# Six stores of normed activations move from ScalarE's queue, in the norm, to the load queue, in the attention

## The chip, the core and the metric

The kernel runs on one core of a Trainium2 chip. A core has five engines that work side by side, each with its own stream of instructions: TensorE (PE in the profile, with its weight loads as PEld), VectorE (DVE), ScalarE (ACT), GpSimd (POOL) and SyncE (SP), which here only issues transfers. Sixteen DMA engines move data between HBM and the on-chip memory SBUF, and within SBUF; a transfer is issued by an instruction on one of the engines' streams. Engines meet at semaphores: an instruction waits until the instructions or transfers that it depends on have counted up.

The metric is the device time of one execution in microseconds, lower is better.

## The reference

The kernel computes one step of a two-layer encoder over 1056 frames (1024 of a prompt, 32 of a sample), 1024 features wide, in float32. Cut to what matters:

```python
def trunk(x, ...):
    for layer in range(DEPTH):                       # 2
        if layer < N_A_LAYERS:                       # layer 0
            mix, C, n, m = mlstm_mixer(x, ...)
        else:                                        # layer 1
            kv = (x @ w_kv).reshape(B, T, 2, N_KV_HEADS, HEAD_DIM)
            k_sh, v_sh = kv[:, :, 0], kv[:, :, 1]
            mix = swa_prompt(x, k_sh, v_sh, w_q_b[j], sinks_b[j], w_out_b[j], slopes)   # or swa_sample
        x = layer_norm(DEEPNORM_ALPHA * x + mix, ln_g[layer, 0], ln_b[layer, 0])
        x = layer_norm(DEEPNORM_ALPHA * x + swiglu(x, w_gu[layer], w_down[layer]), ln_g[layer, 1], ln_b[layer, 1])
    return x, ...

def sink_attention(q, k, v, sinks, bias):
    s = jnp.einsum('bcqhgd,bckhd->bchgqk', q, k) * (HEAD_DIM ** -0.5) + bias
    ...
    return jnp.einsum('bchgqk,bckhd->bcqhgd', p, v)
```

The change lies where layer 0 ends and layer 1 begins: the second `layer_norm` of layer 0 gives the x of which layer 1 makes its keys, values and queries, and which it needs again later, as the residual `DEEPNORM_ALPHA * x + mix`. The attention has 16 query heads of 64 features and two shared key/value heads, over a window of 128 frames.

## The kernel before

**Data.** The activations lie in SBUF in one tile `ACT`, 128 partitions (features within a block) by 8 blocks by 1056 frames; the profile calls it `act`. Float32 products are made of three matmuls on halves: each operand is split into a high half (rounded by ScalarE) and a low half (the rest, by VectorE or GpSimd), and `gemm` adds high·high, low·high and high·low (L402 to L404). The halves of the activations are `SX` (`sx`, L511 and L517), those of the weights `wh` and `wl`, made from the loaded weights `wr` (load L163 on SP, high half L237 on ScalarE, low half L239 mostly on GpSimd).

**The norm (`ln_task`).** It works on quarters of the frames, 264 each. For each quarter it goes through the four pairs of feature blocks: VectorE multiplies by the inverse deviation, ScalarE applies gain and offset (L505), ScalarE writes the high half (L511), VectorE or GpSimd the low half (L517). After the feed-forward part of layer 0 (`li == 1`) a store follows the high half (L513): the attention overwrites `ACT` with its outputs, so the normed values go to `scr` in HBM (`scrx` in the profile) and come back as the residual (`mixed_parts`, L1211 and L1213). Four quarters by four pairs make 16 stores of 264 KB, all issued by ScalarE. They are ScalarE's only transfers.

**The attention.** `keys_values` projects the keys (`k_group`; `k_spread` then copies their halves `KH` and `KL` between partitions, L1623 to L1627 on SP) and the values (`v_group`, transposed by `v_turn`, L1736, and split into `VR`, L1678 and L1679). `q_group(j, g)` projects the queries of pair j of the heads and group g of the frames (groups of 384, 384 and 288): high half `qh` (L1657, ScalarE), low half `ql` (L1658, VectorE), and then four copies on SP which place both into `Q` (L1664 and L1665). `qh` and `ql` have two buffers each, so the third group made waits for the copies of the first. The scores are matmuls of `KH`, `KL` and `Q` (L1763, L1764); VectorE adds the bias `bt` (L1769), whose last column, the sink, GpSimd copies (L1697; L1698 for the sample's `sb`); then come the exponential on ScalarE (L1781), the scaling on GpSimd (L1787), transposes (L1807), products with `VR` (L1822, L1823) and the write to `act` (L1831, L1833).

**What sets the order.** The program is written out in one order for each engine. A class `Weave` holds cooperative tasks: `launch` adds one, `tick(us)` lets an assumed time pass and runs on every task whose pause is over, `drain` runs one to its end. A task yields the pause to its next step. So the pauses in the code fix where in each engine's stream an instruction stands, and nothing is reordered when the kernel runs. Weights are fed by the same ticks. SP's stream holds all loads, the copies within SBUF and the remaining stores; an issue that has to wait holds up everything behind it.

Of the kernel before, what the change touches and what calls it, by code (L numbers as in the profile page):

```python
# [65 lines left out]
HALF = T // 2  # L66
# [216 lines left out]
def kernel(ctx: ExitStack, tc: tile.TileContext, A, O):  # L283
    nc = tc.nc
    ctx.enter_context(tc.manual_schedule())
    wv = Weave()
# [11 lines left out]
    def new(p, tag, shape, dt=F32, bufs=1):  # L298
        uid[0] += 1
        return p.tile(list(shape), dt, name=f"{tag}_{uid[0]}", tag=tag, bufs=bufs)  # L300
# [72 lines left out]
    ACT = base.tile([P, KT, T], F32, name="act")  # L373
# [8 lines left out]
    scr = dram.tile([P, KT, T], F32, name="scrx")  # L382
# [56 lines left out]

    QUARTERS = [(group(g), (g % 2, slice(0, N4))) for g in range(4)]  # L440

    squared, added = set(), set()

    def ln_task(z_, lps, grp, li, last, final):
        cols, (c, zs) = grp
        w = cols.stop - cols.start

        rush = final and grp is QUARTERS[2]
        y = RUSH if rush else LN_PACE[li & 1][last]
        acc = z_[:, 0:2, c, zs]  # L450
        sq = [acc] + [z_[:, 2 + 2 * i : 4 + 2 * i, c, zs] for i in range(3)]
        rs, r2 = z_[:, 8, c, zs], z_[:, 9, c, zs]
        n = KT // 2

        def z2(kk):
            return ACT[:, 2 * kk : 2 * kk + 2, cols]

        def s2(i, kk):
            return SX[:, i, 2 * kk : 2 * kk + 2, cols]

        yield y[0]
        pm = new(lps, "ln", [P, 512], bufs=3 if li & 1 else 2)[:, :w]
        nc.tensor.matmul(pm, onesm[:], acc[:, 0, :], start=True, stop=True)
        yield y[1]
        for s in range(n + 2):
            if s < n:

                nc.vector.tensor_sub(z2(s), pm.unsqueeze(1).broadcast_to([P, 2, w]), z2(s))
            if 1 <= s <= n:
                nc.scalar.activation(sq[s - 1], z2(s - 1), AF.Square)  # L470
            if s >= 3:
                (nc.gpsimd if rush or li & 1 and not (last or s & 1) else nc.vector).tensor_add(acc, acc, sq[s - 2])
            yield y[2]
        if not rush:
            nc.vector.tensor_add(acc[:, 0], acc[:, 0], acc[:, 1])
        added.add((li, cols.start // N4))
        yield y[3] + LN_LAG.get((li, cols.start // N4), 0.0)
        pv = new(lps, "ln", [P, 512], bufs=3 if li & 1 else 2)[:, :w]
        for i in range(1 + rush):
            nc.tensor.matmul(pv, onesm[:], acc[:, i, :], start=(i == 0), stop=(i == rush))  # L480
        squared.add((li, cols.start // N4))
        yield y[4]

        if not li & 1:
            nc.scalar.preload_act_table_set("natural_log_exp_and_others")
        nc.scalar.activation(rs, pv, AF.Ln, bias=eps_ln[:])
        nc.scalar.activation(rs, rs, AF.Exp, scale=-0.5)
        nc.scalar.activation(r2, rs, AF.Square, scale=0.5 ** 0.5)
        yield y[5]
        nc.vector.scalar_tensor_tensor(r2, pv, eps_ln[:], r2, op0=ALU.add, op1=ALU.mult)  # L490
        nc.vector.scalar_tensor_tensor(rs, r2, 1.5, rs, op0=ALU.subtract, op1=ALU.mult)
        if (li, cols.start // N4) == (1, 2):
            while (1, 3) not in added:
                yield 0.2
        for s in range(n + 3):
            if s < n:
                nc.vector.tensor_mul(z2(s), z2(s), rs.unsqueeze(1).broadcast_to([P, 2, w]))
            kk = s - 1
            if 0 <= kk < n:
                for k in (2 * kk, 2 * kk + 1):  # L500
                    z, gk, bk = ACT[:, k, cols], lng[:, li, k : k + 1], lnb[:, li, k : k + 1]
                    if li & 1 and last and k & 1:
                        nc.vector.tensor_scalar(z, z, gk, bk, op0=ALU.mult, op1=ALU.add)
                    else:
                        nc.scalar.activation(z, z, AF.Identity, scale=gk, bias=bk)  # L505
            kk = s - 2
            if 0 <= kk < n:
                if final:
                    nc.sync.dma_start(O["y"][:, 2 * kk : 2 * kk + 2, cols], z2(kk))
                else:  # L510
                    nc.scalar.copy(s2(0, kk), z2(kk))  # L511
                    if li == 1:
                        nc.scalar.dma_start(scr[:, 2 * kk : 2 * kk + 2, cols], z2(kk))  # L513
            kk = s - 3
            if kk >= 0 and not final:
                eng = nc.gpsimd if kk & li & 1 else nc.vector
                eng.tensor_sub(s2(1, kk), z2(kk), s2(0, kk).bitcast(F32))  # L517
            yield y[6]
# [194 lines left out]
    cols = [pa.tile([P, 3, 96], F32, name=f"cols{g}") for g in range(3)]  # L713
# [485 lines left out]
    def mixed_parts(src, free, mixed, pauses):  # L1199


        for g in range(3):
            t0, n = GRP[g]
            while not free(g):
                yield 0.3
            for k in range(KT):
                while not mixed(k, g):
                    yield 0.3
                split_act(k, g)
                if g == 0:  # L1210
                    nc.sync.dma_start(act[k][g], src[:, k, t0 : t0 + n])  # L1211
                elif k % 4 == 3:
                    nc.sync.dma_start(act_g[g][:, k - 3 : k + 1], src[:, k - 3 : k + 1, t0 : t0 + n])  # L1213
                yield pauses[g]
            nparts[0] += 1
# [434 lines left out]
    def q_group(j, g):  # L1650

        t0, n = GRP[g]
        ps = project(U_QB[g > 0][j], g)
        q = Q[j, g] = new(pb, "Q", [P, 2, 384], F32R, bufs=4)
        h, l = (new(pb, tag, [P, 384], F32R, bufs=2)[:, :n] for tag in ("qh", "ql"))
        sc = -(HD ** -0.5)
        nc.scalar.activation(h, ps, AF.Copy, scale=sc)  # L1657
        nc.vector.scalar_tensor_tensor(l, ps, sc, h.bitcast(F32), op0=ALU.mult, op1=ALU.subtract)  # L1658

        def place():  # L1660
            yield 1.0
            for i in range(2):
                own, other = slice(64 * i, 64 * i + 64), slice(64 - 64 * i, 128 - 64 * i)
                nc.sync.dma_start(q[own, i, :n].bitcast(F32), h[own].bitcast(F32))  # L1664
                nc.sync.dma_start(q[other, i, :n].bitcast(F32), l[own].bitcast(F32))  # L1665

        return wv.launch(place())
# [34 lines left out]
    def keys_values(g):  # L1702
        if g == 2:
            k_part(ck[:], SEQ, P)
        for f, w in ((k_group, U_KV[g > 0][0]), (v_group, U_KV[g > 0][1])):
            f(g)
            if g != 1:
                W.done(w)
# [22 lines left out]
    def v_turn(group, pause):  # L1731
        yield pause
        for c, c0, L, g, off in CH:
            if g == group:
                pt = new(psb, "O", [P, 512], bufs=2)
                nc.tensor.transpose(pt[:L, :P], vT[g][:, off : off + L], ident[:])  # L1736
                v_parts(c, pt[:L, :P], L)
                ast["v"] = c + 1
                yield 0.8
# [119 lines left out]
    wv.launch(v_turn(0, 0))  # L1859
    task = wv.launch(attention((GAP_A,) * 8))  # L1860
    ast["ready"] = 4
    for g in range(1, 3):
        keys_values(g)
        wv.launch(v_turn(g, 2.5))
# [8 lines left out]
    def q_made():  # L1873
        yield 4.0
        ast["ready"] += 1

    for i, (j, g) in enumerate(QG):
        if i < 4:
            continue

        while ast["scored"] < 3 * (i - 3):
            wv.tick(0.25)
        q_group(j, g)
        wv.launch(q_made())
        if g == 2:
            W.done(U_QB[1][j])
        if (j, g) == (7, 0):
            nparts[0] = 0
            parts = wv.launch(
                mixed_parts(  # L1890
                    scr,
                    lambda g: ast["ready"] > QG.index((7, g)),
                    lambda k, g: ast["placed"] >= 3 * QG.index((k, g)) + 3,
                    (1.6, 1.0, 1.0),
                )
            )
# [145 lines left out]
```

## Time and profile before

| what | us |
|---|---|
| three timed executions | 2210.44, 2210.89, 2212.62 |
| median | 2210.89 |
| the profiled execution, whole | 2213.98 |
| its span (first to last instruction) | 2212.2 |
| TensorE busy in the span | 2175.5 |
| first and last issue of the stores of L513 | 1134.7, 1197.6 |
| first issue of a load of what they wrote (L1211) | 1342.9 |

Starts in the profile are counted from the span's start. In the rows that follow, an instruction has its start, its length, the engine (a q behind the engine's name: the issue of a transfer), line, operation, output and inputs; in brackets stands how long the engine had been idle and what released it. The chain of work is followed back from a last instruction, at each step to what released it. The transfers of SP take 40.0% of the sixteen DMA engines' span, those of ScalarE 0.6%:

```profile
q1 hardware_dynamic: 169936, 290.94, 40.0%
q10 hardware_dynamic: 4352, 4.33, 0.6%
```

### The profile page before, as it was taken

To read this page: it belongs to the slowest core of one execution; us is meant where nothing else is said; L and a number is where in the kernel's file an instruction comes from. 1 tells how busy PE (TensorE), PEld (TensorE's weight loads), DVE (VectorE), ACT (ScalarE), POOL (GpSimd) and SP (SyncE) were. 2 spreads that over 40 slices of the span, in tenths; PEclk is the share of its full clock that TensorE was granted. 3 is DMA by queue.
4 is the path that set the end of the run, shared out by engine and by line. 5 is a ranking of instruction groups with operands and counts; after the bars stand their busy time and mean duration, and the time that the engine had idled before them with its cause. 6 is when DMAs were issued, how large, how long until landed. Compare 5 with 4: busy or idle time off the path is not lost.

```text
span 2212.2 us, 44257 instructions
## 1 busy us (share of the span) xinstructions
PE 2175.5 (98%) x17086; PEld 2149.4 (97%) x17086; DVE 1455.2 (66%) x2848; ACT 1007.9 (46%) x2259; POOL 989.8 (45%) x982
## 2 busy tenths in 40 slices
PE   9999999999999999999998999999999999999997
PEld 9999999999999999999998999899999999999997
DVE  4465677787656665566667778888666656466657
ACT  4443455464444444321245778756444444432125
POOL 2544210004655555444525776600665555554441
PEclk9999999999999999999999999999999999999999
DMA  5221213212443343797516433511344434397712
GB/s 170 78 62 57 58 40 87 89 39 86 148 156 145 139 147 135 254 329 231 175 57 174 108 100 97 156 63 39 112 161 156 146 127 156 132 344 256 247 56 79
DMA packets 174499, 298.10 MB, mean 135 GB/s; under 512 B 18064, under 2 KB 130760, under 8 KB 174288
## 3 DMA queue, kind: packets, MB, share of 16 engines
q1 hardware_dynamic: 169936, 290.94, 40.0%
q10 hardware_dynamic: 4352, 4.33, 0.6%
q8 instruction: 135, 2.21, 0.4%
q14 instruction: 76, 0.62, 0.1%
HBM read 201.80 MB, written 82.94 MB: 129 GB/s over the span
## 4 chain that ended last, share of the span: by engine, by line
PE 85%; DVE 6%; DMA 3%; ACT 3%; issue 1%; POOL 1%; SPq 0%; ACTq 0%; POOLq 0%; DVEq 0%
PE d L402 10%; PE d L404 10%; PE d L403 10%; PE A L402 9%; PE A L404 9%; PE A L403 9%; PE B L402 7%; PE B L403 7%; PE B L404 7%; DMA sx<-hs_t 1%; PE T L1807 1%; ACT act L505 1%; DMA hs_x<-z 1%; POOL s L1787 1%; PE T L955 1%
## 5 line engine op out<-in xcount | busy, mean ns | idle before, releaser
L239 POOL TENSOR_TENSOR wl_s<-wr,wh_s 128x512 fp32r<-128x512 f32 x224 | 304.1, 1367 | 237.4 <-ACT wh_s L237 168.9
L402 PE MATMUL d<-sx,wh 128*128 128x264 f32 (+2 forms) x1068 | 341.8, 320 | 2.1 <-ACT wh L237 1.8
L239 POOL TENSOR_TENSOR wl_a<-wr,wh_a 128x512 fp32r<-128x512 f32 x112 | 153.5, 1373 | 409.4 <-ACT wh_a L237 288.2
L404 PE MATMUL d<-sx,wl 128*128 128x264 f32 (+2 forms) x1068 | 325.9, 305 | 2.7 <-POOL wl L239 2.7
L403 PE MATMUL d<-sx,wh 128*128 128x264 f32 (+2 forms) x1068 | 325.3, 305 | 0.4 <-DVE sx L433 0.4
L402 PE MATMUL A<-sx,wh_s 128*128 128x264 f32 x896 | 254.7, 284 | 0.0
L403 PE MATMUL A<-sx,wh_s 128*128 128x264 f32 x896 | 254.4, 284 | 0.0
L404 PE MATMUL A<-sx,wl_s 128*128 128x264 f32 x896 | 254.3, 284 | 0.0
L237 ACT CAST wh_s<-wr 128x512 fp32r<-128x512 f32 x224 | 135.7, 618 | 192.6 <-DVE wr L192 102.7
L402 PEld LDWEIGHTS d<-sx,wh 128*128 128x128 f32 x1068 | 202.3, 189 | 5.5 <-ACT wh L237 2.4
L404 PEld LDWEIGHTS d<-sx,wl 128*128 128x128 f32 x1068 | 201.7, 189 | 3.9 <-POOL wl L239 3.6
L403 PEld LDWEIGHTS d<-sx,wh 128*128 128x128 f32 x1068 | 202.6, 190 | 1.5 <-DVE sx L433 0.7
L402 PE MATMUL d<-sx,ex 128*128 128x264 f32 x624 | 180.7, 290 | 0.1
L403 PE MATMUL d<-sx,ex 128*128 128x264 f32 x624 | 177.3, 284 | 0.0
L404 PE MATMUL d<-sx,ex 128*128 128x264 f32 x624 | 177.1, 284 | 0.0
L404 PEld LDWEIGHTS A<-sx,wl_s 128*128 128x128 f32 x896 | 169.0, 189 | 0.0
L402 PEld LDWEIGHTS A<-sx,wh_s 128*128 128x128 f32 x896 | 168.6, 188 | 0.0
L403 PEld LDWEIGHTS A<-sx,wh_s 128*128 128x128 f32 x896 | 168.6, 188 | 0.0
L1323 POOL TENSOR_TENSOR z<-z 128x528 fp32r<-128x528 f32 x76 | 103.2, 1357 | 126.8 <-ACT z L1322 113.3
L239 POOL TENSOR_TENSOR wl<-wr,wh 128x512 fp32r<-128x512 f32 (+2 forms) x81 | 103.9, 1291 | 94.5 <-ACT wh L237 90.7
L1787 POOL TENSOR_SCALAR s<-s,st 128x256 f32<-128x256 f32 (+1 forms) x144 | 122.8, 865 | 46.6 <-DVE st L1785 29.2
L402 PE MATMUL A<-ex,wh_s 128*128 128x264 f32 x448 | 127.5, 285 | 0.0
(352 smaller groups left out, 7247.4 us busy)
## 6 DMA issues: line engine op xcount, KB each, us to landing
wr<-in_gu SPq DMA_DIRECT2D x92, 512.0 KB
hs_x<-z SPq DMA_DIRECT2D x72, 528.0 KB
hs_t<-z SPq DMA_DIRECT2D x64, 528.0 KB
sx<-hs_x SPq DMA_DIRECT2D x112, 264.0 KB
sx<-hs_t SPq DMA_DIRECT2D x64, 264.0 KB
ex<-hs_t SPq DMA_DIRECT2D x64, 264.0 KB
wr<-in_dn SPq DMA_DIRECT2D x32, 512.0 KB
ex<-hs_x SPq DMA_DIRECT2D x32, 264.0 KB
```

The costliest lines, as they stand in the source:

```text
L237: self.nc.scalar.copy(hi, r)
L239: eng.tensor_sub(lo, r, hi.bitcast(F32))
L402: nc.tensor.matmul(out, ah, bh, start=start and k == 0, stop=False, **kw)
L403: nc.tensor.matmul(out, ah, bl, start=False, stop=False, **kw)
L404: nc.tensor.matmul(out, al, bh, start=False, stop=stop and k == last, **kw)
L505: nc.scalar.activation(z, z, AF.Identity, scale=gk, bias=bk)
L955: nc.tensor.matmul(pc[:, : 2 * (DV + 1)], keys, vt[j][:, c], start=True, stop=True)
L1323: eng.tensor_sub(lo.bitcast(F32R), buf(s), hi)
L1787: nc.gpsimd.tensor_scalar_mul(p[:R, h, lo:256], p[:R, h, lo:256], st[:R, 2, h : h + 1])
L1807: nc.tensor.transpose(pt[:nk, i, h, :R], p[:R, h, c : c + nk], ident[:R, :R])
```

## The change

In the third and fourth quarter of the norm after layer 0's feed-forward part, the stores of the first three pairs (k = 0, 2 and 4) are no longer issued. Their places are noted in a list `stores`; the store of the fourth pair stays, as do all stores of the first two quarters. A new task `store`, launched when the attention starts, pauses for 8.0, then issues one noted store on SP for every 2.0 of assumed time; what is left when the first further `q_group` is about to be written is issued there (`drain`). The data stored, and their place in `scr`, are the same.

```diff
-    squared, added = set(), set()
+    squared, added, stores = set(), set(), []
...
                     nc.scalar.copy(s2(0, kk), z2(kk))
                     if li == 1:
-                        nc.scalar.dma_start(scr[:, 2 * kk : 2 * kk + 2, cols], z2(kk))
+                        if kk < n - 1 and cols.start >= HALF:
+                            stores.append((2 * kk, cols))
+                        else:
+                            nc.scalar.dma_start(scr[:, 2 * kk : 2 * kk + 2, cols], z2(kk))
...
     task = wv.launch(attention((GAP_A,) * 8))
     ast["ready"] = 4
+
+    def store():
+        yield 8.0
+        for k, cols in stores:
+            nc.sync.dma_start(scr[:, k : k + 2, cols], ACT[:, k : k + 2, cols])
+            yield 2.0
+
+    storing = wv.launch(store())
     for g in range(1, 3):
         keys_values(g)
         wv.launch(v_turn(g, 2.5))
...
     for i, (j, g) in enumerate(QG):
         if i < 4:
             continue
+        wv.drain(storing)
```

The order of the instructions on TensorE, VectorE and GpSimd is the same before and after. ScalarE loses the six issues. On ScalarE, near the end of the fourth quarter, there stood before:

```order
L511 CAST sx<-act 128x2x264
L513 DMA scrx<-act 128x2x264
L505 ACTIVATE act<-act,lnb,lng 128x264
L511 CAST sx<-act 128x2x264
L513 DMA scrx<-act 128x2x264
L237 CAST wh_0_14205<-wr_14001 128x512
L505 ACTIVATE act<-act,lnb,lng 128x264
L511 CAST sx<-act 128x2x264
L513 DMA scrx<-act 128x2x264
L511 CAST sx<-act 128x2x264
L513 DMA scrx<-act 128x2x264
```

and now:

```order
L511 CAST sx<-act 128x2x264
L505 ACTIVATE act<-act,lnb,lng 128x264
L511 CAST sx<-act 128x2x264
L237 CAST wh_0_14200<-wr_14001 128x512
L505 ACTIVATE act<-act,lnb,lng 128x264
L511 CAST sx<-act 128x2x264 x2
L516 DMA scrx<-act 128x2x264
```

The casts of the first three pairs have no store behind them any more, the last one has; the lines of this part count three higher after the change.

On SP two of the six stores stand earlier in the stream than what follows. The other four stand between the key copies of the third group, the cache outputs and the loads for the first further query group (`bt` and `sb` are bias tables, `wr` weights). On SP there stood before:

```order
L1627 DMA KL_13941<-KL_13941 64x160
L1868 DMA out_p_k<-kout_13947 128x128
L1869 DMA out_s_k<-kout_13947 128x32
L1870 DMA out_p_v<-act 128x128
L1871 DMA out_s_v<-act 128x32
L1689 DMA bt_14718<-in_bias 128x2x256
L1690 DMA sb_14719<-in_bias 32x2x160
L163 DMA wr_14739<-in_wqb 128x1024
L1664 DMA Q_14842<-qh_14843 64x384
L1665 DMA Q_14842<-ql_14844 64x384
```

and now:

```order
L1869 DMA scrx<-act 128x2x264
L1630 DMA KH_13939<-KH_13939 64x256
L1630 DMA KL_13941<-KL_13941 64x256
L1630 DMA KH_13939<-KH_13939 64x160
L1630 DMA KL_13941<-KL_13941 64x160
L1879 DMA out_p_k<-kout_13947 128x128
L1880 DMA out_s_k<-kout_13947 128x32
L1881 DMA out_p_v<-act 128x128
L1882 DMA out_s_v<-act 128x32
L1869 DMA scrx<-act 128x2x264 x3
L1692 DMA bt_14718<-in_bias 128x2x256
L1693 DMA sb_14719<-in_bias 32x2x160
```

One store now stands ahead of the last key copies, and three stand between the last cache output and the bias tables, so ahead of the weights and of the four query copies.

## The prediction

> **What bounds the kernel now.** I read the page's head first, then its chain of work.
>
> ```profile
> span 2212.2 us, 44257 instructions
> PE 2175.5 (98%) x17086; PEld 2149.4 (97%) x17086; DVE 1455.2 (66%) x2848; ACT 1007.9 (46%) x2259; POOL 989.8 (45%) x982
> PE 85%; DVE 6%; DMA 3%; ACT 3%; issue 1%; POOL 1%; SPq 0%; ACTq 0%; POOLq 0%; DVEq 0%
> ```
>
> TensorE (PE) is busy for 2175.5 of 2212.2 us, so only 36.7 us of the span are PE idle time, and a change that leaves PE's instructions alone can only win from those, or add to them. The next question is where the six moved stores stand, and so which of the 36.7 us they could touch. The groups by line and by tile give the stores and their only readers.
>
> ```profile
> L513 ACTq DMA_DIRECT2D scrx<-act x16: 366/366/380, 1134.7 to 1197.6; - x16
> L1211 SPq DMA_DIRECT2D act<-scrx x8: 320/329/608, 1342.9 to 1372.5; - x8
> ```
>
> All sixteen stores are issued from 1134.7 to 1197.6 us, 0.37 us of issue each, and what they wrote is first read at 1342.9, so 100 us later is early enough for all of them; a reader that waits is no concern. Around the place where they leave (up to 1199) and the place where they arrive (1212 to 1240) I read busy time by stretch: start:end, length, then for PE, weight loads, VectorE (DVE), ScalarE (ACT) and GpSimd (POOL) the busy us, then PE's granted clock, the busy share of the 16 DMA engines and GB/s.
>
> ```profile
> 1134.66:1141.06 6.40, 6.40 (x54) 6.40 (x54) 4.50 (x9) 6.09 (x12) 2.56 (x2) 1.00 0.48 172
> 1176.00:1190.00 14.00, 14.00 (x81) 13.94 (x79) 10.78 (x12) 8.87 (x18) 7.66 (x6) 1.00 0.70 197
> 1190.00:1199.00 9.00, 5.31 (x27) 3.98 (x26) 8.96 (x12) 6.88 (x13) 4.52 (x4) 1.00 0.56 177
> 1199.00:1203.00 4.00, 1.20 (x6) 0.88 (x6) 1.63 (x7) 2.13 (x8) 3.81 (x4) 0.91 0.89 253
> 1203.00:1207.00 4.00, 4.00 (x19) 4.00 (x18) 0.47 (x2) 1.09 (x3) 2.65 (x4) 0.66 0.99 250
> 1228.00:1236.00 8.00, 8.00 (x60) 7.92 (x60) 6.45 (x26) 5.91 (x19) 6.85 (x11) 1.00 0.42 125
> 1236.00:1246.00 10.00, 9.41 (x65) 8.64 (x64) 5.74 (x22) 6.41 (x21) 7.22 (x9) 1.00 0.60 142
> 1238.00:1240.00 2.00, 1.81 (x15) 1.79 (x16) 1.69 (x6) 1.30 (x5) 1.13 (x2) 1.00 0.79 172
> 1240.00:1242.00 2.00, 2.00 (x18) 2.00 (x17) 1.36 (x5) 1.66 (x5) 1.31 (x2) 1.00 0.86 275
> ```
>
> The third quarter's stores (before 1190) leave a stretch in which PE has no idle time at all. From 1190 to 1199 PE is idle for 3.69 us, but VectorE is busy for 8.96 of 9.00: the norm is bound by VectorE there. From 1199 on VectorE idles, DMA is at 0.89 and PE at 1.20 of 4.00: here a transfer holds the kernel up, and the fourth quarter's stores are in flight. After it PE runs 4 us at a clock of 0.66. At the far end, 1236 to 1246, PE is nearly full and DMA is not (0.60 overall, yet 0.79 and 0.86 in the middle).
>
> **The change, part by part.**
>
> *Six issues less on ScalarE.* That is 6 × 0.37 = 2.2 us of its queue. Whether it counts is read from two like pairs of ScalarE instructions, the first with a store between them, the second without.
>
> ```profile
> 1184.28 0.62 ACT L511 CAST sx<-act 128x528 fp32r<-128x528 f32 x1
> 1184.41 0.37 ACTq L513 DMA_DIRECT2D scrx<-act  x1
> 1184.80 0.61 ACT L237 CAST wh<-wr 128x512 fp32r<-128x512 f32 x1
> ...
> 1194.74 0.62 ACT L511 CAST sx<-act 128x528 fp32r<-128x528 f32 x1
> 1195.27 0.61 ACT L237 CAST wh<-wr 128x512 fp32r<-128x512 f32 x1
> ```
>
> 0.52 us with the store, 0.53 us without: the issue lies inside the cast. I take 0. The bound on the gain side would be the 2.2 us; it is excluded by these pairs and by VectorE's 8.96 of 9.00. If VectorE were faster, ScalarE (6.88 of 9.00) would still cover it.
>
> *Less DMA traffic before 1202.* Between 1134.66 and 1141.06 almost only four stores run, so one store takes about 6.40 × 0.48 / 4 = 0.77 us of all 16 engines. Three of the fourth quarter's four stores go (the last, for k = 6 and 7, stays): 3 × 0.77 = 2.3 us less beside the loads that PE waits for. Which these are, the chain and the timeline tell (start, length, engine, line; in brackets the idle time before and its releaser; the line with "DMA" is a piece of the chain).
>
> ```profile
> 1195.00 5.22 DMA Q<-qh
> ...
> 1199.18 0.33 PE L404 MATMUL d<-sx,wl 128*128 128x384 f32 x1
> 1200.33 0.49 ACT L1657 ACTIVATE qh<-d 128x384 fp32r<-128x384 f32 x1 [0.70 <-DMA Q<-qh]
> 1201.36 0.56 DVE L1658 SCALAR_TENSOR_TENSOR ql<-d,qh 128x384 fp32r<-128x384 f32 x1 [1.77 <-ACT wh L237]
> 1202.31 0.48 PE L1736 MATMUL O<-ident,act 128*128 128x128 f32 x1 [2.80 <-DVE VR L1679]
> 1203.23 0.52 PE L404 MATMUL d<-sx,wl 128*128 128x384 f32 x1
> 1203.55 0.52 PE L402 MATMUL d<-sx,wh 128*128 128x384 f32 x1
> ...
> 1205.93 0.34 PE L404 MATMUL d<-sx,wl 128*128 128x384 f32 x1
> 1206.11 0.34 PE L402 MATMUL d<-sx,wh 128*128 128x384 f32 x1
> ```
>
> The copy of the high half of Q, issued at 1195.00, lands 5.22 us later and frees a buffer; ScalarE waits 0.70 for it, VectorE writes the low half at 1201.36, and PE, behind both, waits 2.80. With the 2.3 us of DMA gone, ScalarE's 0.70 goes. The low half then starts behind it, and its own buffer is freed by the copy behind this one; between 1200.82, where the high half ends, and 1201.36 there are 0.54 us that can go too. So PE's wait falls by 0.70 to 1.24; I take 1.2, since both copies stand in the same traffic. The lower end is 0 (the Q copies also queue behind the weight load issued before them), the upper the 2.80 whole. After the wait come about eleven matmuls 0.32 us apart instead of 0.18: 11 × 0.14 = 1.5 us that would also go if the wait got too short to lower the clock. But then another engine is next:
>
> ```profile
> 1205.36 0.19 POOL L1697 COPY bt<-nsink 128x2 f32<-128x2 f32 x1
> 1207.30 0.28 DVE L1769 CUSTOM_DVE_ANT_0 s<-psS,bt 128x129 f32<-128x129 f32 x1
> ```
>
> The first score step on VectorE (1207.30) needs the bias column that GpSimd copies at 1205.36, behind its weight halves; GpSimd is 3.81 of 4.00 busy before. The scores can't start before 1205.55 + 0.1: together the two gains are worth at most 1.6 us here. I take −1.2 (the clock as before), ends 0 and −1.6; without GpSimd's bound it would be −2.8 − 1.5 = −4.3.
>
> *Six issues more on SP, the load queue.* The first two arrive in idle time of SP, I cost them at 0. The third stands among the key copies, the last three between the cache outputs and the loads of the next Q group (pair 0, frames 384 to 767). There the queue works without a pause:
>
> ```profile
> 1236.55 0.43 SPq L1871 DMA_DIRECT2D out_s_v<-act  x1
> 1237.03 0.43 SPq L1689 DMA_DIRECT2D bt<-in_bias  x1
> 1237.50 0.47 SPq L1690 DMA_DIRECT2D sb<-in_bias  x1
> 1238.07 0.37 SPq L163 DMA_DIRECT2D wr<-in_wqb  x1
> 1238.55 0.47 SPq L1664 DMA_DIRECT2D Q<-qh  x1
> 1240.73 0.59 SPq L1665 DMA_DIRECT2D Q<-ql  x1
> 1240.73 4.61 DMA Q<-ql
> ...
> 1245.47 0.36 PE L1763 MATMUL psS<-KH,Q 128*128 128x256 f32 x1 [0.17 <-DMA Q<-ql]
> ```
>
> One issue follows the other every 0.47 us. Four more push everything behind them by 4 × 0.47 = 1.9 us: the bias tables, the next weights wr, and the four Q copies, the last of which lands at 1240.73 + 4.61 = 1245.34, and PE's score matmuls wait for just that. Against it stands the 1.2 us by which the whole queue starts earlier: Q is issued 0.7 us later than before. Then the transfers: three stores are 2.3 us of DMA; while they are issued, 3 × 0.47 = 1.4 us of it drain; 0.9 us are still in front of wr and Q, where DMA is at 0.79 and 0.86 and has no room. So Q lands 0.7 + 0.9 = 1.6 us later than before, and all of it reaches PE, which already waited there. Ends: −1.2 (the stores hide in the 4.0 us that DMA is idle from 1236 to 1246, and SP catches up), and +1.9 + 2.3 = +4.2 (nothing gained earlier, nothing drained). The 0.9 is the softest term; I take it because the two rows of 1238 to 1242 are the nearest.
>
> *PE's clock at the new wait.* PE's wait in front of these scores grows by 1.2 (PE arrives earlier) and 1.6, from about 0.4 to 3.2 us. The rows above show a wait of 2.80 us followed by eleven matmuls at 0.32 instead of 0.18, so another 1.5 us may follow here; the lower end is 0. I take 0, because 1.20 us of PE work in 1199 to 1203 left the clock at 0.91 and it fell only later, so where the wait lies counts as well as its length. The Trainium skill, "TensorE: Matmul & The Clock Gate", section "What's actually happening", puts the drop behind an idle window of about 3.4 us, free-running. By it alone neither 2.80 nor 3.2 us would have to lower the clock; the trace shows 0.66 after 2.80, so the measurement decides, and the sum by the page would be +1.6, by the row +3.1.
>
> **Sum.** 0 − 1.2 + (1.2 + 1.6) + 0 = +1.6 us, since the −1.2 is inside the wait that takes its place. The profiled execution took 2213.98 us, 1.8 over its span; it would be 2215.6. It stands 3.1 above the median of 2210.89, and the three timed executions spread from 2210.44 to 2212.62; on the median the forecast is 2210.89 + 1.6 = 2212.5. 0.2% is 4.4 us, about what a measurement of this kernel can tell from no change.
>
> **The rivals.**
>
> *The gain is kept (faster).* The wr load that stands before Q lands without queueing, the stores hide, and Q is on time: −1.2 to −1.6, 2209.5. For it speaks DMA's 0.42 from 1228 to 1236; against it that PE already waits for Q in the row of 1245.47. In its large form GpSimd's copy also moves up, because its weight halves wait for ScalarE, which is freed at 1199: then 2.80 of wait and 1.5 of half clock go, −4.3, and with some of the 3.69 us of PE idle before 1199 it passes 0.2%: 2206.
>
> *Q of the next group is late by all of it (slower).* Place: SP's run of issues at 1236 to 1241. Price: 1.9 of issue and 2.3 of transfer with no gain at 1202 (the Q copies there wait for the weight load anyway), +4.2, and 1.5 for a half-clock stretch behind a wait of 4.6 us: +5.7, 2216.6. It decides once Q lands over 2.9 us later than 1245.34 and the clock falls too. For it speaks the chain, in which the copies of Q carry both places; against it the 4.0 us in which DMA is idle there.
>
> *Nothing happens.* The same bytes pass the same 16 engines, only later; if the Q copies at 1195 queue behind the weight load alone, and the stores at 1237 ride beside wr, both terms are 0: 2210.9. The mechanism here would be that the copies issued at 1195.00 land 5.2 us later with or without the stores. This is also the Trainium skill's view in "DMA: Bandwidth & Descriptors", section "Issuing engines are not separate DMA queues": transfers of all issuing engines run on the same 16 engines and interleave, and the issuer changes only the sequencer's time. The L1211 row's late readers agree that nothing else hangs on them; the trace alone can't show the landing without the stores.
>
> **How the numbers follow.** Given back at the next Q group (+0 to +3.1): 0.42, the forecast. Nothing: 0.08. Gain kept small: 0.12, large: 0.12. Q late by all: 0.26. Only the large gain is faster by over 0.2% (0.12), only the last slower (0.26), the rest within (0.62). The range runs from the large gain, 2206.0, to the late Q, rounded up to 2217.0. The likeliest case's own range is 2210.9 to 2214.0.
>
> **What would show it.** In the profile after: ScalarE's wait at qh (0.70) gone and PE's 2.80 at 1202 at about 1.6; the clock row of 1203 to 1207 tells whether the half-clock stretch went too. SP's Q copies of that group issued near 1241.4 with the three stores just ahead; PE's wait before the score matmuls there near 3 us. If that wait stays under 0.5 us and the 2.80 is shorter, the gain is kept. If the 2.80 is unchanged, the stores were not what delayed Q. What would make the forecast wrong is a wait that the order of issue can't show: a store's slot or a buffer released late, in front of SP's loads at 1212 to 1240, or a clock stretch elsewhere that appears or goes because all later work shifts by a microsecond or two.

## The result and the profile after

The changed kernel takes 2216.3 us in the median (2213.0 to 2219.0, ten executions) against 2210.9 before (2210.3 to 2212.6): the ratio is 1.0020, with a 95% interval of 1.0011 to 1.0029, or 2.4 to 6.4 us more. A second comparison gave 1.0012 (1.0003 to 1.0020). So the change makes the kernel slower, by some 3 to 4 us, at the edge of the 0.2% that the prediction took as the bound of "within".

Two lines of the page of after:

```profile
span 2214.3 us, 44263 instructions
PE 2178.0 (98%) x17086; PEld 2151.3 (97%) x17086; DVE 1452.9 (66%) x2848; ACT 1007.8 (46%) x2259; POOL 991.8 (45%) x982
```

TensorE has the same 17086 matmuls, and is busy 2.5 us longer: the same work, partly at a lower clock. Two further profiles of before have 2174.5 and 2177.0, so this difference is no larger than theirs. Busy time by stretch, with the columns of the prediction, after:

```profile
1190.00:1199.00 9.00, 4.96 (x25) 3.81 (x24) 8.32 (x14) 6.00 (x13) 4.34 (x4) 0.92 0.50 140
1199.00:1203.00 4.00, 4.00 (x14) 3.73 (x15) 2.02 (x7) 2.52 (x7) 4.00 (x3) 0.50 0.17 58
1203.00:1207.00 4.00, 4.00 (x22) 4.00 (x22) 0.81 (x3) 1.26 (x3) 4.00 (x6) 0.82 0.92 250
...
1236.00:1246.00 10.00, 8.07 (x57) 7.47 (x55) 5.03 (x19) 6.00 (x19) 7.20 (x9) 1.00 0.83 225
```

Where the stores left, DMA fell from 0.89 to 0.17 (1199 to 1203), and PE, which had worked for 1.20 of these 4 us, now works for all 4.00, but at a clock of 0.50. Most of this first difference belongs to the one execution: in two further profiles of before, DMA is at 0.59 and 0.46 there and PE works for all 4.00 us; in two of after DMA is at 0.40 and 0.22. Where the stores arrived, DMA rose from 0.60 (0.61 and 0.54 in the further profiles) to 0.83 (0.87 and 0.88), and PE fell from 9.41 to 8.07 us of 10. SP's timeline of after at that place:

```profile
1231.70 0.59 SPq L1869 DMA_DIRECT2D scrx<-act  x1
...
1236.36 0.44 SPq L1882 DMA_DIRECT2D out_s_v<-act  x1
1236.84 1.49 SPq L1869 DMA_DIRECT2D scrx<-act  x3
1238.38 0.50 SPq L1692 DMA_DIRECT2D bt<-in_bias  x1
1238.92 0.69 SPq L1693 DMA_DIRECT2D sb<-in_bias  x1
1239.71 0.40 SPq L163 DMA_DIRECT2D wr<-in_wqb  x1
1240.22 0.47 SPq L1667 DMA_DIRECT2D Q<-qh  x1
...
1242.02 0.62 SPq L1668 DMA_DIRECT2D Q<-ql  x1
```

The last of the four query copies is issued at 1242.02, and by the chain of after it takes longer than before:

```profile
1242.02 5.29 DMA Q<-ql
```

It lands at 1242.02 + 5.29 = 1247.31, against 1245.34 before. PE, in the timeline, had finished what it could at 1244.3; here are its two waits for the queries, and then the first of the two of before (the other, at 1245.47, is 0.17):

```profile
1246.55 0.39 PE L1766 MATMUL psS<-KH,Q 128*128 128x256 f32 x1 [2.25 <-DMA Q<-ql]
...
1247.45 0.35 PE L1766 MATMUL psS<-KH,Q 128*128 128x256 f32 x1 [0.40 <-DMA Q<-ql]
```

```profile
1244.80 0.39 PE L1763 MATMUL psS<-KH,Q 128*128 128x256 f32 x1 [0.19 <-DMA Q<-ql]
```

That is 2.65 us of waiting in place of 0.36.

**Stages that can be compared.** Since the order on PE is the same in both kernels, its n-th matmul is the same work, and the time between two of them can be set side by side over all profiled executions, whatever happened earlier. I cut at the matmuls that start at 1189.65, 1206.11, 1244.27 and 1261.84 in the first profile of before: A is the end of the norm with the first queries, where the stores left; B runs up to the last matmul ahead of the scores of the first further query group; C goes from there over these scores. (In us; the experiments are told below. For two executions of before and two of after the profile was taken again.)

| execution | A | B | C | A+B+C | half-clock stretches in A to C |
|---|---|---|---|---|---|
| before, first profile | 16.46 | 38.16 | 17.57 | 72.19 | 1202 |
| before, second | 13.78 | 38.16 | 17.00 | 68.94 | 1199 |
| before, third | 13.81 | 39.70 | 16.90 | 70.41 | 1197, 1225 |
| after, first | 14.72 | 38.18 | 19.86 | 72.77 | 1198 (double) |
| after, second | 14.78 | 38.20 | 19.64 | 72.62 | 1197 (double) |
| after, third | 14.65 | 38.15 | 22.59 | 75.39 | 1197 (double), 1248 |
| only the fourth quarter moved | 13.43 | 38.16 | 17.10 | 68.70 | 1199 |
| only the third moved | 14.65 | 38.17 | 17.40 | 70.22 | 1198 (double) |
| last three behind the query copies | 13.79 | 38.18 | 17.05 | 69.01 | 1202 |
| six issued early, none on SP | 14.58 | 38.19 | 16.91 | 69.68 | 1196 (double) |
| doubled | 12.85 | 39.72 | 18.51 | 71.08 | 1224 |
| on ScalarE in the attention | 14.88 | 39.46 | 16.88 | 71.23 | 1197 (double) |
| short stores on SP | 13.67 | 39.72 | 17.83 | 71.22 | 1198, 1225 |
| three merged into one | 13.76 | 39.71 | 16.91 | 70.38 | 1198, 1225 |

Over the three profiles each, before takes 70.5 us and after 73.6: 3.1 us more, as the medians say. C carries it: 17.2 before, 20.7 after. The first profile of before stands out in A, by 2.7 us. Against the other two, after is also 0.9 us longer in A, with a double stretch of half clock; the run that has this too but no store on SP ("six issued early") is no slower than before, as told below. An extra stretch at 1225 adds 1.5 us to B in before as well as in experiments, so it is not the change's.

### The profile page after: what moved, and what is told of

The parts are those of the page before. It is cut to its first block, busy times and chain, and to the rows that moved or that the text cites. A ratio compares the mean times of both kernels' runs of the same rounds, so it can differ in the third digit from the quotient of the medians.

```text
span 2214.3 us, 44263 instructions
## 1 busy us (share of the span) xinstructions
PE 2178.0 (98%) x17086; PEld 2151.3 (97%) x17086; DVE 1452.9 (66%) x2848; ACT 1007.8 (46%) x2259; POOL 991.8 (45%) x982
## 4 chain that ended last, share of the span: by engine, by line
PE 86%; DVE 5%; DMA 3%; ACT 3%; POOL 1%; issue 1%; SPq 0%; POOLq 0%; ACTq 0%; DVEq 0%
PE d L402 10%; PE d L404 10%; PE d L403 10%; PE A L402 9%; PE A L404 9%; PE A L403 9%; PE B L402 7%; PE B L403 7%; PE B L404 7%; DMA sx<-hs_t 1%; PE T L1810 1%; POOL wl L239 1%; DMA sx<-hs_x 1%; DMA hs_x<-z 1%; PE O L1825 1%
```

## The experiments

Theory 1: the loss is in stage C, because the first further query group stands behind four stores in SP's queue. Theory 2: it comes from stage A, where the stores left. Times are against before on the same chip, with the ratio's 95% interval. The expectations count from the 2210.9 us of before; beside the runs below it took 2212.2 in the median, and 2211.6 beside the last two, so the ratio is what tells.

**Only the fourth quarter's stores move.**

```diff
-                        if kk < n - 1 and cols.start >= HALF:
+                        if kk < n - 1 and cols.start > HALF:
```

> Only the three stores of the fourth quarter move to the load queue; those of the third stay on ScalarE. Theory 1 (the loads of the first further query group stand behind four stores on SP): one store is left in SP's run of issues, so the last of these query copies lands less than 1 us later than its 1245.3 before, against 1247.3 after, and PE's wait there is 0.4 to 1.4 us against 2.65; the copies at 1195 still land by 1198.5 as after. Time 2208 to 2212, against 2216.3 after. Theory 2 (the loss comes where the stores leave, because the stretch of half clock moves from 1202 to 1197): the fourth quarter is what leaves, so the loss stays, 2214 to 2217.

Measured: ratio 0.9998 (0.9989 to 1.0006), 2211.1 us. The three stores now take the three early places in SP's stream, and none is left between the cache outputs and the bias tables; one stays ahead of the last key copies. SP's timeline of this run:

```profile
1228.92 1.10 SPq L1869 DMA_DIRECT2D scrx<-act  x1
...
1234.08 0.43 SPq L1882 DMA_DIRECT2D out_s_v<-act  x1
1234.55 0.43 SPq L1692 DMA_DIRECT2D bt<-in_bias  x1
...
1238.19 0.59 SPq L1668 DMA_DIRECT2D Q<-ql  x1
```

PE ran 2.53 us ahead of the first profile of before here, and 1238.19 + 2.53 = 1240.72 is, against PE's work, the very place at which before issued this copy (1240.73): the one store ahead of the key copies cost the queries nothing. C is 17.10, as in before, and PE does not wait at the scores (0.4 to 1.4 us had been expected). Theory 2 asked for 2214 to 2217 and falls.

**Only the third quarter's stores move.**

```diff
-                        if kk < n - 1 and cols.start >= HALF:
+                        if kk < n - 1 and cols.start == HALF:
```

> Only the three stores of the third quarter move; those of the fourth stay on ScalarE. Both theories: PE's wait of about 2.8 us near 1202 comes back. Theory 1: with one store in SP's run the time is that of before up to 1.2 us more, 2210 to 2213. Theory 2: the time of before, 2210 to 2212. A theory 3 (the gain is ScalarE's stall at 1188.8 to 1190.2, in front of a store that waits for its slot): 1 to 1.5 us faster than before, 2209 to 2210, since the issues whose slots it waits for are the third quarter's.

Measured: 1.0005 (0.9997 to 1.0014), 2213.5 us. By the ratio that is 1.1 us more than before (−0.7 to +3.1), which both theory 1 (up to 1.2) and theory 2 (0) allow; theory 3 (faster than before) falls. But one expectation that both shared is missed: the 2.8 us of waiting near 1202 did not come back, though the fourth quarter's stores were on ScalarE again. That was the first sign that this wait does not belong to the kernel.

**The last three stores behind the query copies.**

```diff
-        for k, cols in stores:
+        for i, (k, cols) in enumerate(stores):
+            while i > 2 and not ast.get("first"):
+                yield 0.5
...
-        wv.drain(storing)
...
-        q_group(j, g)
+        placing = q_group(j, g)
+        if i == 4:
+            wv.drain(placing)
+            ast["first"] = 1
+            wv.drain(storing)
```

> All six move as in the change, but the last three are issued behind the four query copies of the first further group instead of ahead of the bias tables. Theory 1: the query copies land within 0.8 us of 1245.3, PE's wait there is 0.4 to 1.2 us, the next group's copies may land up to 2 us later but PE has other work then; time 2208 to 2212. Theory 2: 2214 to 2217, as after. A theory 4 (any 2.3 us of DMA work near 1240 costs, wherever it stands): 2213 to 2216, with a wait of 1.5 to 2.5 us at the next group's scores.

Measured: 0.9999 (0.9990 to 1.0008), 2212.5 us. SP's timeline, then PE's, of this run:

```profile
1237.47 0.43 SPq L1692 DMA_DIRECT2D bt<-in_bias  x1
...
1241.09 0.59 SPq L1668 DMA_DIRECT2D Q<-ql  x1
1241.72 1.76 SPq L1871 DMA_DIRECT2D scrx<-act  x3
1245.24 0.34 SPq L163 DMA_DIRECT2D wr<-in_wqb  x1
```

```profile
1244.65 0.34 PE L404 MATMUL d<-sx,wl 128*128 128x384 f32 x1
1244.87 0.36 PE L1766 MATMUL psS<-KH,Q 128*128 128x256 f32 x1
```

The same stores, the same bytes, some 4 us later in the same queue: PE goes from the weights' matmuls to the scores without a wait, C is 17.05, and the loss is gone. This is the plainest evidence for theory 1. Theory 4 (that 2.3 us of transfers cost wherever they stand here) falls with it: PE has no such wait anywhere in C.

**The relief without the cost.** All six stores are issued by ScalarE in the first two quarters, and none in the attention; the kernel leaves out storing the right values for these places.

```diff
-                        if kk < n - 1 and cols.start >= HALF:
-                            stores.append((2 * kk, cols))
-                        else:
+                        if kk == n - 1 or cols.start < HALF:
                             nc.scalar.dma_start(scr[:, 2 * kk : 2 * kk + 2, cols], z2(kk))
+                        if kk < n - 1 and cols.start < HALF:
+                            late = slice(cols.start + HALF, cols.stop + HALF)
+                            nc.scalar.dma_start(scr[:, 2 * kk : 2 * kk + 2, late], z2(kk))
```

> The gain without the cost: nothing is issued on SP, and the six stores are issued by ScalarE during the first two quarters, right behind those quarters' own stores, with the first quarters' data (so the residual of the third and fourth quarter is wrong in three of four pairs of blocks; the work is the same). Theory 1: PE's wait of 2.8 us near 1202 shrinks below 1.2 us, the query wait near 1245 stays 0.2 to 0.8 us; 1.2 to 3.5 us faster than before, 2207.5 to 2210. Theory 2: as slow as after, 2214 to 2217. No gain there at all: 2210 to 2212.

Measured: 0.9999 (0.9990 to 1.0008), 2212.5 us. I had expected a gain of 1.2 us or more; there is none. Stage C is free of the wait (16.91), so what failed is the gain in A (14.58, no better than the 13.8 of before's second and third profile, told next).

**Before, profiled again**, to see why.

> The kernel before, unchanged, profiled a second time, to see what of its rows repeats. If the wait of 2.80 us at 1202 and the half-clock stretch behind it belong to the kernel, both come again within 0.5 us, and the stretch from 1190 to 1262 takes as long as in the first profile (72.2 us) within 0.5 us. If they are an accident of the free-running clock, that stretch is 1 to 3 us shorter, which is why the first profiled execution stands 1.8 to 3.1 us above the medians.

The PE timeline of this second profile:

```profile
1192.73 0.44 PE L404 MATMUL d<-sx,wl 128*128 128x384 f32 x1 [0.93 <-POOL wl L239]
...
1197.09 0.44 PE L402 MATMUL d<-sx,wh 128*128 128x384 f32 x1 [2.35 <-ACT wh L237]
...
1198.68 0.45 PE L404 MATMUL d<-sx,wl 128*128 128x384 f32 x1 [0.97 <-POOL wl L239]
```

No wait at 1202 at all. PE waits at 1197 for the high half of a weight tile, and ScalarE, which makes it, is held by VectorE (ScalarE's and VectorE's timelines of the same profile):

```profile
1193.28 0.61 ACT L505 ACTIVATE act<-act,lnb,lng 128x264 f32<-128x264 f32 x1 [2.53 <-DVE act L497]
```

```profile
1191.59 1.66 DVE L497 TENSOR_TENSOR act<-act,z 128x528 f32<-128x528 f32 x1
```

What set the first profile apart is in its ScalarE rows at the end of the third quarter:

```profile
1188.15 0.62 ACT L511 CAST sx<-act 128x528 fp32r<-128x528 f32 x1
1190.19 0.37 ACTq L513 DMA_DIRECT2D scrx<-act  x1
1190.61 0.49 ACT L1657 ACTIVATE qh<-d 128x384 fp32r<-128x384 f32 x1 [1.84 <-PE d L404]
1190.99 0.61 ACT L237 CAST wh<-wr 128x512 fp32r<-128x512 f32 x1
```

The cast ended at 1188.77, and the store behind it was issued only at 1190.19, 1.4 us later; ScalarE stood idle for 1.84. The transfers of this kernel share eight semaphores, and one that is given a semaphore which an earlier transfer still counts up waits for that one to land. In the trace this store shares semaphore 108 with the weight load that SP had issued at 1183.71. By the trace's DMA events that load was complete at 1190.17, 6.46 us after its issue, where the same load took 4.10 and 4.15 us in the second and third profile. There too the store was issued 0.02 us behind the load's landing, but that was before the cast had ended (in the second profile at 1188.91), and ScalarE did not stop.

What the held store did further on is read from the rows, and no run shows it by itself. The load and the four query copies behind it were issued later, beside the stores of the fourth quarter, and the copies took 5.00, 4.85, 5.22 and 5.60 us to land, against 4.29, 3.88, 3.89 and 4.22 in the second profile; PE's 2.80 us followed. The same store was held in two experiments which also keep the third quarter's stores on ScalarE. With only the fourth quarter moved, the load took 5.48 us, ScalarE stood idle for 0.86 and PE did not wait at this place. In the run told below as doubled, which has the fourth quarter's stores there too, it took 5.89 us, and PE waited 0.72:

```profile
1190.39 0.49 ACT L1659 ACTIVATE qh<-d 128x384 fp32r<-128x384 f32 x1 [1.26 <-DMA wr<-in_wqb]
```

So in three of the six executions that keep these stores on ScalarE a slow load stopped it, and in the slowest one the weights, the query copies and PE were late with it. The 72.2 us of the stretch became 68.9, a little more of a fall than the 1 to 3 us of the expectation's second case, and not for its reason: a stretch of half clock is there again, at 1199.

> The kernel before, unchanged, a third profile. The wait of 2.80 us at 1202 was absent in the second; if the first was the exception, it is absent again, the copies issued near 1195 land by 1199.5, and PE waits 2.2 to 2.5 us near 1197 for the high half of a weight tile instead. If it comes and goes, 1 to 3 us are seen at 1202 again.

The third profile agrees: no wait at 1202, 2.32 us at 1195.7 on the weight tile's high half, 2211.99 us. The 2.80 us were the exception among the three.

**After, profiled again.**

> The changed kernel, unchanged, profiled a second time, beside the other kernels on the same chip. Theory 1 (the first further query group stands behind four stores on SP): the copies land 1.5 to 2.5 us later than in the kernel before, PE's wait at their scores is 2 to 3.2 us again; in some executions a half-clock stretch follows. Ratio 1.001 to 1.003.

Measured: 1.0012 (1.0003 to 1.0020), 2214.4 us; the waits at the scores are 1.87 and 0.56 us.

> The changed kernel, unchanged, a third profile: PE's wait at the scores of the first further query group 1.8 to 2.8 us, the copies issued near 1195 landing by 1198.5, a stretch of half clock between 1196 and 1204.

The third profile, 2218.68 us, shows the upper end of what after does. Its PE timeline:

```profile
1246.60 0.38 PE L1766 MATMUL psS<-KH,Q 128*128 128x256 f32 x1 [3.18 <-DMA Q<-ql]
...
1247.80 0.49 PE L1766 MATMUL psS<-KH,Q 128*128 128x256 f32 x1 [0.70 <-DMA Q<-ql]
...
1248.31 0.52 PE L402 MATMUL d<-sx,wh 128*128 128x384 f32 x1
1248.63 0.52 PE L403 MATMUL d<-sx,wh 128*128 128x384 f32 x1
```

3.88 us of waiting, more than the 2.8 expected, and behind it a stretch at half clock: 0.32 us from one matmul to the next. C is 22.59, or 18.71 without the waits, where the first two profiles of after have 17.21 (19.86 − 2.65 and 19.64 − 2.43): 1.5 us is the slower clock. The copies near 1195 and the stretch between 1196 and 1204 came as expected.

**The cost without the relief.** ScalarE keeps all sixteen stores, and SP issues the six a second time.

```diff
                         if kk < n - 1 and cols.start >= HALF:
                             stores.append((2 * kk, cols))
-                        else:
-                            nc.scalar.dma_start(scr[:, 2 * kk : 2 * kk + 2, cols], z2(kk))
+                        nc.scalar.dma_start(scr[:, 2 * kk : 2 * kk + 2, cols], z2(kk))
```

> The cost without the relief: all sixteen stores stay on ScalarE in the norm, and SP issues the six a second time, at the places where the change has them. Theory 1: as slow as after or up to 1.5 us slower, 2214 to 2219; PE's wait at the query scores 2 to 3.5 us. If the loss came from the place where the stores leave: the time of before, 2210 to 2213.

Measured: 1.0013 (1.0004 to 1.0021), 2214.1 us, as slow as after. So the relief is worth nothing that can be measured from this side either. The wait in its profile is shorter than expected:

```profile
1244.32 0.35 PE L1765 MATMUL psS<-KH,Q 128*128 128x256 f32 x1 [1.37 <-DMA Q<-qh]
```

In this execution a half-clock stretch fell at 1224, PE came 1.55 us later (B is 39.72), and the queue caught up part of its delay meanwhile.

**The same places, issued by ScalarE.**

```diff
-            nc.sync.dma_start(scr[:, k : k + 2, cols], ACT[:, k : k + 2, cols])
+            nc.scalar.dma_start(scr[:, k : k + 2, cols], ACT[:, k : k + 2, cols])
```

> The same six stores at the same places of the attention, but issued by ScalarE, so that SP's run of issues is that of before and only the transfers are added. If SP's issue time and the order within its queue make the loss: PE's wait at the query scores is 0.2 to 1 us, 2209 to 2213. If the 2.3 us of transfers beside the loads make it: 2213.5 to 2217, with a wait of 1.5 to 2.6 us. A cost on ScalarE itself: three issues together take 1.1 us of it ahead of exponentials; that would show as a later first exponential after 1236, and could add up to 1 us to either.

Measured: 1.0009 (1.0000 to 1.0018), 2214.6 us. The wait for the queries is gone (C 16.88). But on ScalarE's stream the three stores came earlier, and by the trace's DMA events they had landed by 1234.3, ahead of the weight load at 1237.2; so this run does not show what the same transfers do beside the queries. And ScalarE pays, 8 us ahead of where I had looked for it:

```profile
1228.34 1.74 ACTq L1869 DMA_DIRECT2D scrx<-act  x3
1230.13 0.51 ACT L1784 ACTIVATE s<-s,st 128x257 f32<-128x257 f32 x1 [1.90 <-DMA KL<-KL]
```

The exponential behind the three stores starts at 1230.13; in before's second profile, 0.1 us ahead of this run there, it starts at 1228.00. By the trace each of the three stores was issued 0.02 us behind the landing of an earlier transfer on its semaphore: a weight load and two key copies. B is 1.3 us longer.

**Issues or transfers.** First the six extra issues with an eighth of the bytes (16 of the 128 partitions; ScalarE keeps all stores):

```diff
-            nc.sync.dma_start(scr[:, k : k + 2, cols], ACT[:, k : k + 2, cols])
+            nc.sync.dma_start(scr[:16, k : k + 2, cols], ACT[:16, k : k + 2, cols])
```

> All sixteen stores stay on ScalarE; SP issues six more, at the places of the change, but of only 16 of the 128 partitions (33 KB instead of 264 KB each). So SP has the same number of issues more and an eighth of the transfers. If SP's issues make the loss (4 x 0.47 = 1.9 us): the query copies are issued as late as after, PE's wait at their scores is 1 to 2.2 us, 1.0 to 2.5 us slower than before. If the transfers in front of them in the same queue make it: wait below 0.8 us, within 1 us of before.

Measured: 1.0013 (1.0004 to 1.0022), 2214.0 us. Almost without bytes there is a loss (0.9 to 4.9 us), and nothing tells it from after's. In the profile the three issues take nearly the time of after's (1.36 against 1.49 us), and the wait is 0.61 us:

```profile
1235.09 1.36 SPq L1868 DMA_DIRECT2D scrx<-act  x3
1236.49 0.42 SPq L1691 DMA_DIRECT2D bt<-in_bias  x1
...
1239.82 0.59 SPq L1667 DMA_DIRECT2D Q<-ql  x1
```

```profile
1244.20 0.35 PE L1765 MATMUL psS<-KH,Q 128*128 128x256 f32 x1 [0.61 <-DMA Q<-qh]
```

Here too a half-clock stretch at 1225 made PE 1.55 us later, so this one profile can't tell the two readings apart (its wait is below the 0.8 that the transfers' theory asked for). The median, 2.4 us above before, lies outside that theory's 1 us and speaks for the issues, but the interval begins at 0.9.

Then the same bytes with two issues less:

```diff
-        for k, cols in stores:
-            nc.sync.dma_start(scr[:, k : k + 2, cols], ACT[:, k : k + 2, cols])
+        for i, (k, cols) in enumerate(stores[:4]):
+            e = k + (2 if i < 3 else 6)
+            nc.sync.dma_start(scr[:, k:e, cols], ACT[:, k:e, cols])
```

> As the change, but the three stores that stand together in front of the bias tables are one transfer of 792 KB: the same bytes at the same place with one issue instead of three, so 0.9 to 1.0 us less of SP's time. If SP's issues make the loss: the copies land about 1 us earlier than after, wait 1 to 1.7 us instead of 1.9 to 2.7, 1.5 us slower than before or less. If the transfers make it: the wait stays 1.9 to 2.7 us and the ratio 1.001 to 1.002.

Measured: 1.0009 (1.0000 to 1.0018), 2213.6 us. The interval holds both expectations; its profile had the stretch at 1225 as well and no wait at the scores, so the time settles nothing. SP's own rows say more:

```profile
1233.94 0.43 SPq L1883 DMA_DIRECT2D out_s_v<-act  x1
1234.42 0.43 SPq L1870 DMA_DIRECT2D scrx<-act  x1
1234.89 0.54 SPq L1692 DMA_DIRECT2D bt<-in_bias  x1
1235.48 1.13 SPq L1693 DMA_DIRECT2D sb<-in_bias  x1
1236.71 0.45 SPq L163 DMA_DIRECT2D wr<-in_wqb  x1
```

From the last cache output to the weight load it is 2.77 us here. It is 1.52 in each of the three profiles of before, 3.35 in each of the three of after, and 2.92 with the short stores. So the three stores hold SP for 1.83 us with all their bytes, for 1.40 with an eighth of them, and one issue with all the bytes still for 1.25, since the issue behind it takes 1.13 instead of 0.47. Together: SP's issues are enough to make a loss, the bytes lengthen the issues behind them, and how the kernel's time divides between the two stays open.

No kernel here beats before by what can be measured.

## Why the prediction was right and wrong

The measured time lies in the range and on the side that was forecast, but the +1.6 us are about half the loss: the two comparisons gave +4.4 and +2.7. By its steps:

*Six issues less on ScalarE: 0.* Right. Without them anywhere late (the early stores) the time is that of before within 2 us. The step's reason missed one thing: a store can also hold ScalarE while it waits for its semaphore, as the 1.4 us of the first profile show; the store that did so stays in the changed kernel, where it has another semaphore and was not held in its three profiles.

*Less DMA traffic before 1202: −1.2.* This is the step that failed. The traffic fell, though by less than the first profiles show (DMA 0.89, 0.59 and 0.46 in before, 0.17, 0.40 and 0.22 in after), and the last of the query copies issued near 1195 landed sooner, 3.30, 3.56 and 3.26 us after its issue instead of 4.22 and 4.11. But PE's 2.80 us of waiting, which are not in after, are not in the second and third profile of before either, so there is nothing to win: stage A takes 13.8 us there and 14.7 in after. The relief alone measured 0; its interval, −2.2 to +1.8 us, does not exclude a gain of 1.2, and it is the profiles that decide. The number came from one execution that stood 3.1 us over the median, and an excess of 2.7 was in just this place; I set the profile's own time beside the median and did not ask where the 3.1 us were.

The step's bound, that the gain can't pass 1.6 us because the first score step waits for GpSimd's copy of the bias column, is a wrong reading too. In the second profile of before the score step starts ahead of that copy, which so can't be what it waits for:

```profile
1205.73 0.28 DVE L1769 CUSTOM_DVE_ANT_0 s<-psS,bt 128x129 f32<-128x129 f32 x1
```

```profile
1206.56 0.19 POOL L1697 COPY bt<-nsink 128x2 f32<-128x2 f32 x1
```

*Six issues more on SP: +1.6 against before.* Place and mechanism are right: four issues, three transfers, the last query copy, PE's wait. Counted from PE's own progress, the last copy was issued 1.6, 1.5 and 1.9 us later in the three profiles of after than in the first of before; 4 × 0.47 = 1.9 was forecast for the issues. From issue to landing it took 5.29, 5.22 and 6.25 us, against 4.61: 0.6 to 1.6 more, where 0.9 was forecast. Without the −1.2 the step's own terms give 1.9 + 0.9 = 2.8; C grew by 2.3, 2.1 and 5.0 us over the first profile of before. Inside, the terms lie otherwise. The store ahead of the key copies cost nothing, the three others 0.61 us each in place of 0.47. The weight load ahead of the query copies took as long to land as before (6.04, 5.96 and 6.27 us, against 5.96 and 5.95 in the first two profiles of before), so the stores' transfers hardly stood in its way; it was issued later. And the queue did not quite work without a pause: in before SP idles for 0.56 us behind the first query copy, ahead of a row that the prediction left out, and that time took up part of the delay:

```profile
1239.57 0.47 SPq L1665 DMA_DIRECT2D Q<-ql  x1
```

*The first two stores on SP cost 0.* Borne out: no wait is seen at them, and B is that of before in all three profiles of after (38.15 to 38.20 against 38.16).

*PE's clock at the new wait: 0, at most 1.5.* It followed in one of three profiles, after 3.88 us of waiting, at 1.5 us, the upper end; not after 2.65 and 2.43. So the value taken is right for two of three executions.

*The sum.* +1.6 forecast, +2.7 and +4.4 measured. The mis-sized terms are the relief (0, not −1.2) and, in part of the executions, the clock. That the forecast came out on the right side does not rest on the relief: without it the sum is +2.8.

*The rivals.* A kept gain and a change that does nothing fall: the wait at the scores is there in each of the three profiles. "Late by all of it" was right that nothing is gained at 1202 and that a half-clock stretch can follow; its +4.2 was reached in one profile of three. The truth lies between the forecast and this rival.

*The clock's rule* of the Trainium skill, "TensorE: Matmul & The Clock Gate", section "What's actually happening" (half clock behind an idle window of about 3.4 us), is neither borne out nor refuted here. 2.65 us of waiting was followed by full clock and 3.88 by half; but the first profile's 2.80 was followed by half, and so were the waits of 2.3 us in stage A of eleven of the fourteen executions. So the length of the last wait alone does not tell.

## What to carry to other kernels

Before a gain is taken from a wait in one profile, ask whether that execution stands above the median of the timed ones, and by how much: a wait that is about as long as the excess may be the excess. A second profile of the same kernel told here what the first could not. A transfer without a hurry belongs behind the hurried ones of the same queue, not ahead of them; the same three stores cost 3 us in front of four small copies and nothing right behind them. In a queue that works almost without pauses both count, the number of issues and their bytes: what stood behind the three stores was issued 1.83 us later, 1.40 with an eighth of the bytes, 1.25 with one issue for all of them.

## What was not expected

Half-clock stretches came in pieces of 3.41 us, one or two of them together, in each of the fourteen profiled executions somewhere between 1196 and 1252, often behind waits of PE that were alike. In stage A a double piece cost about 0.9 us over a single one (14.6 to 14.9 against 13.4 to 13.8, the first profile of before with its other delay left out). It appeared in all three profiles of after, and in three of the five experiments in which the third quarter's stores left the norm, and in none of the six executions in which they stayed. Whether the change brings the double piece, or it fell so by chance, is open; the relief alone, which shows it, is no slower than before.

A weight load that took 6.46 us in one execution and 4.1 in two others stopped ScalarE for 1.84 us, and nearly 3 us of PE's waiting came with it: a semaphore shared between a store and an unrelated load ties one to the other. The same tie held the stores on ScalarE in the attention.
